# A longer first product after side work, and other places for two sets of split weights, in a two-layer decoder kernel on one core

## The chip, the cores and the metric

The kernel runs on one core of a Trainium2 chip. The metric is the device time of one execution in microseconds (us), as the median of several runs. The core has a matrix engine (PE in the profile; its loading of the stationary operand is a row of its own, PEld), a vector engine (DVE), a scalar engine (ACT), GpSimd (POOL), a queue that issues transfers (SP), and 16 DMA engines. The engines run their own instruction streams and wait for one another by semaphores.

## The reference

A sequence of 256 tokens of width 2048 goes through two layers. Each is a mixer followed by a layer norm over a scaled residual.

```
layer 0 (state space):   z, xBC, dt = split(x @ w_in)           # 2048 -> 4096 + 6144 + 64
                         xBC = silu(causal_conv4(xBC)); xs, B, C = split(xBC)
                         y = chunked scan of (xs, dt, B, C), 8 groups of 8 heads of 64; + d_skip * xs
                         h = group_rms_norm(y * silu(z)) @ w_out  # 4096 -> 2048
layer 1 (sparse attn):   c_q 512, c_kv 256, k_idx 64, w_idx 16, gate 4096 = split(x @ w_in)
                         rms-normed c_q -> 32 query heads, and 16 index heads; top 64 keys per token
                         latent attention over the chosen rows of c_kv; o * silu(gate) @ w_out
x = layer_norm(4**0.25 * x + h) after each layer
```

All is in float32. Nothing of this is changed.

## The kernel before, in words

**Products in three parts.** Each float32 matrix is split into two halves of precision, hi and lo, in a type that the matrix engine takes in one pass. A product a·w is then three products: hi·hi, hi·lo, lo·hi. Weights come from memory in blocks of 128 rows by up to 1024 columns ("units"). For each unit SP issues one transfer into `raw`, ACT copies it to `hi` (L109), DVE subtracts to get `lo` (L131), and PE multiplies. `Stream.run` goes through the list of units in order: it has the unit four ahead converted, calls the unit's `pe`, and then lets each running piece of side work take one step. So the order of the program is written out by hand: a unit's products, then one step of each side piece, then the next unit.

**Where the split weights lie.** `Stream.places` takes a buffer of 1088 columns for hi and one for lo, in rotation over four, and hands out a part of it. Units whose weights stay in the array (`STILL`) start at column 16 (64 bytes); units whose weights are streamed through it (`MOVING`) start at column 0; `KEYS` units have two halves with a gap. `homes` gives single units buffers from another pool and a column to start at. The last four units of the program have `homes` at column 48 (192 bytes).

**The projections by `stream_w`.** The input projection of layer 0 (tile `acc`, moving operand `xT`) and the gates of layer 1 (tile `g`, moving operand `x1T`) have two units for each block of 128 output columns. For each unit the stationary operand is a 128x128 piece of hi or lo, and the moving operand is 256 columns (all tokens): 16 products with hi (L321; hi and lo of the activations alternate) and 8 with lo (L317). The hi and lo activations of one row block lie side by side, 256 columns each. The result tile has 512 columns, of which 256 are used. One group of layer 0 has 10 blocks, so 20 units.

**The side work on PE.** Between units stand short float32 products: the transposed step sizes (`p_dtt`, L291 and L294, once), B·C (`cb`, L365 and L366), transposes of the channel tiles (`pxs`, L416), the scan's outputs (`y`, L436, by `y_steps`, two halves per group), and the mean squares (`ms`, L464). In layer 1 they are the transposes of the normed latents (`qt`, `kvt`, L759), of the index key (`kdt`, L780), index scores (`sa`, `sb`), logits (`lg`), their transposes (`pt`) and outputs (`o`). With `y` of half 0 of a group a run of 10 units follows without side work; with `cb`, `pxs` and `y` of half 1 one of 5.

**Latents.** `stream_tok` multiplies tokens by the 512 columns of c_q (`qp`) and by the 336 of c_kv, k_idx and w_idx (`kvp`, L690 to L692; weights moving). A `kvp` unit holds two row blocks of 336 columns, one behind the other: the second begins 1344 bytes after the first.

**The end.** The output projection (`o`, L537 to L539, 512 columns wide) holds its last 8 units back for the second half of the tokens. The last four of these are done in two passes of 256 columns, into `o` and `part`; then two short sums (`c`, L1210 and L1213) and four vector operations end the program.

Of the kernel before, what the change touches and what calls it, by code (L numbers as in the profile page):

```python
# [17 lines left out]
T = 256  # L18
# [38 lines left out]

MOVING, STILL, KEYS = range(3)  # L60


class Unit:
# [6 lines left out]
class Stream:  # L70


    def __init__(self, nc, wraw, whi, wlo):
        self.nc, self.wraw, self.whi, self.wlo = nc, wraw, whi, wlo
        self.units, self.starts, self.active, self.behind = [], {}, [], []
        self.raws, self.parts, self.halfway = {}, {}, {}
        self.pos = self.ready = 0
        self.limit = 1 << 30
        self.homes = {}

    def add(self, src, width, pe, use):
        self.units.append(Unit(src, width, pe, use))
# [13 lines left out]
    def convert(self, i, eng, later=False):  # L96

        if i < len(self.units):
            u = self.units[i]
            r = self.raws.pop(i)  # L100
            h, l = self.places(i)
            r = r[:, :u.width]
            if u.use == KEYS:
                r = r.rearrange("p (a b) -> p a b", a=2)
            elif i == 0:
                self.nc.scalar.activation(h[:, 0:512], r[:, 0:512], AF.Copy)  # L106
                self.nc.scalar.activation(h[:, 512:1024], r[:, 512:1024], AF.Copy)
            if i:
                self.nc.scalar.activation(h, r, AF.Copy)  # L109
            self.halfway[i] = l, r, h.bitcast(F32)  # L110
            self.parts[i] = (h, l)
        if not later:
            self.finish(i, eng)

    def places(self, i):

        u = self.units[i]
        if i in self.homes:
            pool, o = self.homes[i]
            t = [pool.tile([P, 1088], F32R, tag=k, name=f"{k}{i}") for k in ("hi", "lo")]  # L120
        else:
            o = 16 if u.use == STILL else 0
            t = [pool.tile([P, 1088], F32R, tag=k, name=f"{k}{i}")
                 for pool, k in ((self.whi, "hi"), (self.wlo, "lo"))]
        if u.use == KEYS:
            return [a.rearrange("p (a b) -> p a b", a=2)[:, :, 32:544] for a in t]
        return [a[:, o:o + u.width] for a in t]

    def finish(self, i, eng):
# [34 lines left out]
def trunk_kernel(ctx: ExitStack, tc: tile.TileContext, x, xt, w1, wdt, dtp, prm, wo1,  # L164
                 wkv, wcq, wix, wg, wab, wo2, lnr, out):
    nc = tc.nc
# [21 lines left out]
    def m_tile(name):  # L188
        return p_m.tile([P, 512], F32, tag="m", name=name)
# [68 lines left out]
    def dt_steps():  # L258
# [28 lines left out]
        nc.gpsimd.dma_start(acs_d, acs)  # L287
        yield
        yield
        pt = m_tile("p_dtt")  # L290
        nc.tensor.transpose(pt[:, 0:P], dtT, ident)  # L291
        for h in range(2):
# [10 lines left out]
    def stream_w(half, cell, name, turn=True):  # L303


        def pe(h, l):
            if half == 0:
                cell["ps"] = acc_tile(name)[:, 0:T]
            ps, xs = cell["ps"], cell["x"][0]
            first, second = (1, 0) if half and turn else (0, 1)  # L310
            for lo in (first, second):
                for k in range(8):
                    kt = half * 8 + k
                    last = half == 1 and lo == second and k == 7
                    wt = (l if lo else h)[:, k * P:(k + 1) * P]
                    if lo:
                        nc.tensor.matmul(ps, wt, xs[:, kt, 0:T], start=False,  # L317
                                         stop=last, skip_group_check=True)
                    else:
                        for c in range(2):  # L320
                            nc.tensor.matmul(ps, wt, xs[:, kt, c * T:(c + 1) * T],  # L321
                                             start=(kt == 0 and c == 0), stop=last and c == 1,
                                             skip_group_check=True)
        return pe

    G = [dict() for _ in range(NG)]
# [1 line left out]

    def conv_steps(g, kind, ci, cc, cell):

        ps = cell["ps"]
        acc = sp3.tile([P, T], F32, tag="cacc", name=f"ca{cc}")

        def w(k):
            return convh[:, cc * 5 + k:cc * 5 + k + 1]
        nc.scalar.activation(acc, ps, AF.Identity, scale=w(3), bias=w(4))
        yield
        for k in (2, 1, 0):
            d = 3 - k
            v.scalar_tensor_tensor(acc[:, d:], ps[:, :T - d], w(k), acc[:, d:],  # L340
                                   op0=ALU.mult, op1=ALU.add)
        yield
        if kind == "x":
            dst = sp2.tile([P, T], F32, tag="xs", name=f"xs{g}_{ci}", bufs=12)
        else:
            dst = sp1.tile([P, T], F32, tag=kind, name=f"{kind}{g}")
        nc.scalar.activation(dst, acc, AF.Tanh)
        yield
        v.scalar_tensor_tensor(dst, dst, 1.0, acc, op0=ALU.add, op1=ALU.mult)
        G[g][(kind, ci)] = dst  # L350
        yield

    def z_steps(g, ci, cell):
        ps = cell["ps"]
        zs = sp2.tile([P, T], F32, tag="zs", name=f"zs{g}_{ci}", bufs=4)
        nc.scalar.activation(zs, ps, AF.Tanh, scale=0.5)
        yield
        v.scalar_tensor_tensor(zs, zs, 1.0, ps, op0=ALU.add, op1=ALU.mult)
        G[g][("z", ci)] = zs
        yield  # L360
# [48 lines left out]
    def xst_steps(g, half):  # L409

        xsT = sp2.tile([P, 2, 2, P], F32, tag="xsT", name=f"xsT{g}_{half}")
        pm = m_tile(f"pxs{g}_{half}")
        for c in (0, 1):
            for s in (0, 1):
# [10 lines left out]

    def y_steps(g, half):

        py = y_tile(f"y{g}_{half}")
        xsT = G[g][("xsT", half)]
        ms = [G[g].pop(("M", 2 * half + c)) for c in (0, 1)]  # L430
# [220 lines left out]
    v.tensor_scalar_mul(convh, convh, 0.5)  # L651
    st.run(n_ssd + 27)
    ssd.close()


    d1 = ctx.enter_context(tc.tile_pool(name="d1", bufs=1))
# [24 lines left out]
    def stream_tok(kb, width, cell, name, held=None):  # L681

        def mm(kb, h, l, half):
            ps = cell["ps"][half][:, 0:width]
            for k in range(2):
                kt = kb * 2 + k
                ah = X1[0][:, kt, half * P:(half + 1) * P]
                al = X1[0][:, kt, T + half * P:T + (half + 1) * P]
                hs, ls = h[:, k * width:(k + 1) * width], l[:, k * width:(k + 1) * width]
                nc.tensor.matmul(ps, ah, hs, start=(kt == 0), stop=False)  # L690
                nc.tensor.matmul(ps, ah, ls, start=False, stop=False)
                nc.tensor.matmul(ps, al, hs, start=False, stop=(kt == 15))  # L692
# [17 lines left out]
    GT = {}  # L710

    def gate_steps(h, cell):
        ps, d2 = cell["ps"], L["d2"]
        if h < 16:
            g = A["gates"][h]
        else:
# [16 lines left out]
    def lat_norm(cell, width, g0, nt, name, dst):  # L733
# [17 lines left out]
        yield  # L751
        yield
        for q in range(nt // 2):
            pm = m_tile(f"{name}t{q}")
            for k in range(2):
                for half in range(2):
# [13 lines left out]
    def kidx_steps(cell):  # L770
# [4 lines left out]
            v.tensor_copy(kd[:, :, k * 64:(k + 1) * 64], tok[:, :, 256:320])  # L775
        yield
        yield
        pm = m_tile("kdt")
        for half in range(2):
            nc.tensor.transpose(pm[:, half * P:(half + 1) * P], kd[:, half, :], ident)  # L780
# [8 lines left out]
                                             held if kb < EARLY else None), MOVING)  # L789
    st.side(i, (lat_norm, cells["q"], 512, PC_QG, 4, "q", "cqT"))  # L790
    for kb in range(8):
        i = st.add(wkv[kb], 672, stream_tok(kb, 336, cells["kv"], "kvp"), MOVING)
    st.side(i, (lat_norm, cells["kv"], 256, PC_KVG, 2, "kv", "ckvT"))
    st.side(i, (kidx_steps, cells["kv"]))
    gates = iter(range(NH2))
# [461 lines left out]
    heads.close()  # L1257
    wmore = ctx.enter_context(tc.tile_pool(name="wlast", bufs=4))
    for i in range(len(st.units) - 4, len(st.units)):
        st.homes[i] = wmore, 48  # L1260
    st.run(len(st.units))
    st.drain()

# [80 lines left out]
```

## Time and profile before

| | |
|---|---|
| runs | 1232.03, 1232.05, 1232.72 us; median 1232.05 |
| the profiled execution | 1232.59 us, of which the span from first to last instruction is 1230.3 us |
| DMA queue of the weights | 215.29 MB, 54.7% of 16 engines' span |
| DVE L131, the lo halves | 404 instructions, 491.7 us |
| ACT L109, the hi halves | 403 instructions, 421.8 us |
| PE L321 and L317 into `acc` | 2560 and 1280 products, 477.7 us busy |
| PE L321 and L317 into `g` | 1024 and 512 products, 196.9 us busy |

A row of the timeline gives the start in us from the span's start, the length, engine, line and operation, out<-in, the shape (weights, then moving operand) and how many instructions are merged. Products are pipelined: the length of one is more than its step, so the time of a product is read from the difference of two starts, divided by the count between them. The windows view gives the busy time of each engine in a stretch.

### The profile page before, as it was taken

Reading aid. Unit: us, or ns where it says so; the run is one execution under the profiler, and the core shown is the slowest. Engines: PE = TensorE matmul, PEld = TensorE weight load, DVE = VectorE, ACT = ScalarE, POOL = GpSimd, SP = SyncE. Lnnn points to the kernel's source line nnn. Section 1 sums busy time; section 2 is a strip of 40 time slices with the busy share of each in tenths; the row PEclk is TensorE's granted clock in tenths of the full one; section 3 lists DMA queues with packets and bytes.
Section 4 is the critical chain, followed back from the end, with each engine's and each line's share of the span. In section 5 each row is a group of like instructions: output and inputs, shape, how many; then the busy total and the mean of one; then the engine's idle time right before and its main releaser. Section 6 shows DMA issues by size and latency. Waiting matters only on the chain.

```text
span 1230.3 us, 22861 instructions
## 1 busy us (share of the span) xinstructions
PE 1224.1 (99%) x8981; PEld 1141.6 (93%) x8981; DVE 902.9 (73%) x1644; ACT 667.7 (54%) x1163; POOL 65.1 (5%) x102
## 2 busy tenths in 40 slices
PE   9999999999999999999999999999999999999998
PEld 8999999999999999888888899999999999888886
DVE  7878787887888888756556767877777777567457
ACT  5555555665566556444335655566666666433441
POOL 0001011001100110110000000000000001000000
PEclk9999999999999999999999999999999999999999
DMA  8665566566656665667656564554544555875662
GB/s 296 226 187 192 192 196 196 168 217 194 192 174 208 202 193 175 190 212 245 196 193 205 184 216 148 179 172 155 163 149 154 168 156 186 314 228 186 200 195 94
DMA packets 65370, 236.75 MB, mean 192 GB/s; under 512 B 8024, under 2 KB 8160, under 8 KB 64880
## 3 DMA queue, kind: packets, MB, share of 16 engines
q1 hardware_dynamic: 60352, 215.29, 54.7%
q0 software_dynamic: 4912, 20.02, 4.9%
q8 instruction: 70, 1.15, 0.4%
q14 instruction: 36, 0.29, 0.1%
HBM read 231.00 MB, written 4.28 MB: 191 GB/s over the span
## 4 chain that ended last, share of the span: by engine, by line
PE 99%; DMA 1%; DVE 0%; SPq 0%; ACT 0%; DVEq 0%; issue 0%
PE acc L321 24%; PE acc L317 12%; PE g L321 10%; PE o L537 9%; PE o L538 9%; PE o L539 9%; PE g L317 5%; PE y L436 2%; PE q L892 1%; PE q L894 1%; PE q L893 1%; PE pt L957 1%; PE v L880 1%; PE v L881 1%; PE v L879 1%; PE k L870 1%
## 5 line engine op out<-in xcount | busy, mean ns | idle before, releaser
L131 DVE TENSOR_TENSOR lo<-raw,hi 128x1024 fp32r<-128x1024 f32 (+1 forms) x404 | 491.7, 1220 | 271.7 <-ACT hi L109 270.8
L109 ACT ACTIVATE hi<-raw 128x1024 fp32r<-128x1024 f32 (+1 forms) x403 | 421.8, 1051 | 214.9 <-PE o L539 157.4
L321 PE MATMUL acc<-xT,hi 128*128 128x256 f32 x2560 | 314.2, 279 | 0.2 <-ACT hi L106 0.2
L321 PEld LDWEIGHTS acc<-xT,hi 128*128 128x128 f32 x2560 | 303.3, 188 | 3.3 <-ACT E L391 1.2
L317 PE MATMUL acc<-xT,lo 128*128 128x256 f32 x1280 | 163.5, 279 | 0.0
L317 PEld LDWEIGHTS acc<-xT,lo 128*128 128x128 f32 x1280 | 154.7, 188 | 0.1
L321 PE MATMUL g<-x1T,hi 128*128 128x256 f32 x1024 | 126.7, 278 | 0.0
L321 PEld LDWEIGHTS g<-x1T,hi 128*128 128x128 f32 x1024 | 120.7, 188 | 0.2
L537 PE MATMUL o<-hi,yg 128*128 128x512 f32 x256 | 100.3, 392 | 0.0
L537 PE MATMUL o<-hi,og 128*128 128x512 f32 (+1 forms) x256 | 99.7, 389 | 0.0
L539 PE MATMUL o<-hi,yg 128*128 128x512 f32 x256 | 99.7, 389 | 0.0
L538 PE MATMUL o<-lo,yg 128*128 128x512 f32 x256 | 99.6, 389 | 0.0
L539 PE MATMUL o<-hi,og 128*128 128x512 f32 (+1 forms) x256 | 98.9, 386 | 0.0
L538 PE MATMUL o<-lo,og 128*128 128x512 f32 (+1 forms) x256 | 98.8, 386 | 0.0
L340 DVE SCALAR_TENSOR_TENSOR ca<-acc,par,ca 128x255 f32<-128x255 f32 x144 | 69.0, 479 | 3.4
L317 PE MATMUL g<-x1T,lo 128*128 128x256 f32 x512 | 70.2, 281 | 0.0
L317 PEld LDWEIGHTS g<-x1T,lo 128*128 128x128 f32 x512 | 62.9, 188 | 0.2
L537 PEld LDWEIGHTS o<-hi,yg 128*128 128x128 f32 x256 | 48.1, 188 | 10.2 <-ACT hi L109 0.2
L539 PEld LDWEIGHTS o<-hi,yg 128*128 128x128 f32 x256 | 48.0, 188 | 10.1
L538 PEld LDWEIGHTS o<-lo,yg 128*128 128x128 f32 x256 | 48.1, 188 | 9.7
L539 PEld LDWEIGHTS o<-hi,og 128*128 128x128 f32 x256 | 48.1, 188 | 9.7
L538 PEld LDWEIGHTS o<-lo,og 128*128 128x128 f32 x256 | 48.1, 188 | 9.6
(270 smaller groups left out, 1660.6 us busy)
## 6 DMA issues: line engine op xcount, KB each, us to landing
raw<-in_w_dram SPq DMA_DIRECT2D x160, 512.0 KB, 3.8
raw<-in_wo_dram SPq DMA_DIRECT2D x128, 512.0 KB, 4.2
raw<-in_wg_dram SPq DMA_DIRECT2D x64, 512.0 KB, 3.5
raw<-in_wab_dram SPq DMA_DIRECT2D x32, 512.0 KB, 3.5
abc<-acs_d POOLq DMA_DIRECT2D x32, 256.0 KB, 4.2
raw<-in_wcq_dram SPq DMA_DIRECT2D x8, 512.0 KB, 4.5
raw<-in_wkv_dram SPq DMA_DIRECT2D x8, 336.0 KB, 3.3
scr<-in_xt_dram SPq DMA_DIRECT2D x4, 512.0 KB, 6.3
```

The lines of the kernel that those rows point to most:

```text
L109: self.nc.scalar.activation(h, r, AF.Copy)
L131: eng.tensor_sub(*self.halfway.pop(i))
L317: nc.tensor.matmul(ps, wt, xs[:, kt, 0:T], start=False, stop=last, skip_group_check=True)
L321: nc.tensor.matmul(ps, wt, xs[:, kt, c * T:(c + 1) * T], start=(kt == 0 and c == 0), stop=last and c == 1, skip_group_check=True)
L340: v.scalar_tensor_tensor(acc[:, d:], ps[:, :T - d], w(k), acc[:, d:], op0=ALU.mult, op1=ALU.add)
L436: nc.tensor.matmul(py[ks, c * T + s * P:(c + 1) * T], xsT[:, s, c, ks], ms[c][k][:, ws], start=(c == 0 and s == 0), stop=(s == 1), skip_gr ...
L537: nc.tensor.matmul(ps, ah, hs, start=(kk == 2 * first), stop=False)
L538: nc.tensor.matmul(ps, ah, ls, start=False, stop=False)
L539: nc.tensor.matmul(ps, al, hs, start=False, stop=(kk == 31))
L870: nc.tensor.matmul(ps, h[:, 0, o:o + P], ckvT[:, ct, 0:T], start=(ct == 0), stop=False)
L879: nc.tensor.matmul(ps, ch, h[:, 1, o:o + T], start=(ct == 0), stop=False)
L880: nc.tensor.matmul(ps, ch, l[:, 1, o:o + T], start=False, stop=False)
```

## The change

A field `wide` of the stream tells `stream_w` how many columns the next unit's first product takes on top of its 256; it is used once and set back to 0. Pieces of side work set it: 16 at the program's start and behind `p_dtt`, 96 behind every `y` and behind the first `pxs` of group 0 (0 behind any other `pxs`), 64 when layer 0's pools are closed and behind `qt`, `kvt` and `kdt`. The longer product reads on into the columns that lie behind its operand and writes into columns of the result tile that nothing reads; only its first 256 columns are used, as before.

The `kvp` units get a kind of their own, `TWO`: the two row blocks start at bytes 64 and 1472 of the buffer in place of 0 and 1344. The last four units start at byte 0 of their home in place of 192.

```
+MOVING, STILL, KEYS, TWO = range(4)
...
+        self.wide = 16
...
-            if u.use == KEYS:
+            if u.use in (KEYS, TWO):
                 r = r.rearrange("p (a b) -> p a b", a=2)
...
+        if u.use == TWO:
+            return [a[:, o + 16:o + 720].rearrange("p (a b) -> p a b", a=2)[:, :, 0:336] for a in t]
...
     def dt_steps():
...
+        st.wide = 16
         pt = m_tile("p_dtt")
...
         def pe(h, l):
             if half == 0:
-                cell["ps"] = acc_tile(name)[:, 0:T]
+                cell["ps"] = acc_tile(name)
             ps, xs = cell["ps"], cell["x"][0]
             first, second = (1, 0) if half and turn else (0, 1)
+            n, st.wide = T + st.wide, 0
             for lo in (first, second):
                 for k in range(8):
                     kt = half * 8 + k
                     last = half == 1 and lo == second and k == 7
                     wt = (l if lo else h)[:, k * P:(k + 1) * P]
-                    if lo:
-                        nc.tensor.matmul(ps, wt, xs[:, kt, 0:T], start=False,
-                                         stop=last, skip_group_check=True)
-                    else:
-                        for c in range(2):
-                            nc.tensor.matmul(ps, wt, xs[:, kt, c * T:(c + 1) * T],
-                                             start=(kt == 0 and c == 0), stop=last and c == 1,
-                                             skip_group_check=True)
+                    for c in (range(1) if lo else range(2)):
+                        nc.tensor.matmul(ps[:, 0:n], wt, xs[:, kt, c * T:c * T + n],
+                                         start=(kt == 0 and not lo and c == 0),
+                                         stop=last and c == (1 - lo), skip_group_check=True)
+                        n = T
...
     def xst_steps(g, half):
...
+        st.wide = 96 if g == half == 0 else 0
...
     def y_steps(g, half):
+        st.wide = 96
...
     ssd.close()
+    st.wide = 64
...
     def stream_tok(kb, width, cell, name, held=None):
...
-                hs, ls = h[:, k * width:(k + 1) * width], l[:, k * width:(k + 1) * width]
+                hs, ls = (w[:, k * 512:(k + 1) * 512] if width == 512 else w[:, k, :]
+                          for w in (h, l))
...
         for q in range(nt // 2):
+            st.wide = 64
             pm = m_tile(f"{name}t{q}")
...
+        st.wide = 64
         pm = m_tile("kdt")
...
-        i = st.add(wkv[kb], 672, stream_tok(kb, 336, cells["kv"], "kvp"), MOVING)
+        i = st.add(wkv[kb], 672, stream_tok(kb, 336, cells["kv"], "kvp"), TWO)
...
-        st.homes[i] = wmore, 48
+        st.homes[i] = wmore, 0
```

No instruction changes its engine or its place. In all 19 products get longer: 14 behind `y` and one behind `pxs` by 96 columns, two by 64, two by 16. On PE, the place behind `y` of half 0 of group 0 reads as follows before. `y` is the scan's output tile; `acc` is a block of the input projection, and the hi and lo tiles are split weights.

```order
L436 MATMUL y_0_1095<-M_802,xsT_0_720 64x128
L436 MATMUL y_0_1095<-M_982,xsT_0_720 64x256
L436 MATMUL y_0_1095<-M_984,xsT_0_720 64x256
L436 MATMUL y_0_1095<-M_982,xsT_0_720 64x128
L436 MATMUL y_0_1095<-M_984,xsT_0_720 64x128
L321 MATMUL acc_1110<-xT,hi_989 128x256 x16
L317 MATMUL acc_1110<-xT,lo_990 128x256 x8
```

The same place on PE in the changed kernel:

```order
L440 MATMUL y_0_1095<-M_802,xsT_0_720 64x128
L440 MATMUL y_0_1095<-M_982,xsT_0_720 64x256
L440 MATMUL y_0_1095<-M_984,xsT_0_720 64x256
L440 MATMUL y_0_1095<-M_982,xsT_0_720 64x128
L440 MATMUL y_0_1095<-M_984,xsT_0_720 64x128
L322 MATMUL acc_1110<-xT,hi_989 128x352
L322 MATMUL acc_1110<-xT,hi_989 128x256 x15
L322 MATMUL acc_1110<-xT,lo_990 128x256 x8
```

One product of the sixteen is 352 columns wide; the rest stands as it did. On PE at the start of layer 1's gates, behind the `kvp` products and behind `kdt`, before:

```order
L692 MATMUL kvp_8219<-hi_8324,x1T 128x336
L321 MATMUL g_8419<-x1T,hi_8347 128x256 x16
L317 MATMUL g_8419<-x1T,lo_8348 128x256 x8
L317 MATMUL g_8419<-x1T,lo_8370 128x256 x8
L321 MATMUL g_8419<-x1T,hi_8369 128x256 x16
L321 MATMUL g_8501<-x1T,hi_8387 128x256 x16
L317 MATMUL g_8501<-x1T,lo_8388 128x256 x8
L759 MATMUL kvt_8526<-ident,sC 128x128 x4
L780 MATMUL kdt<-ident,sC 128x128 x2
L317 MATMUL g_8501<-x1T,lo_8414 128x256 x8
```

The same place on PE in the changed kernel:

```order
L698 MATMUL kvp_8219<-hi_8324,x1T 128x336
L322 MATMUL g_8419<-x1T,hi_8347 128x320
L322 MATMUL g_8419<-x1T,hi_8347 128x256 x15
L322 MATMUL g_8419<-x1T,lo_8348 128x256 x8
L322 MATMUL g_8419<-x1T,lo_8370 128x256 x8
L322 MATMUL g_8419<-x1T,hi_8369 128x256 x16
L322 MATMUL g_8501<-x1T,hi_8387 128x256 x16
L322 MATMUL g_8501<-x1T,lo_8388 128x256 x8
L766 MATMUL kvt_8526<-ident,sC 128x128 x4
L788 MATMUL kdt<-ident,sC 128x128 x2
L322 MATMUL g_8501<-x1T,lo_8414 128x320
L322 MATMUL g_8501<-x1T,lo_8414 128x256 x7
```

The first product of each of the two runs of gates is 320 columns wide, the second of them one with a lo half.

More of the change, by code (lines that the diff above doesn't have):

```diff
@@ L55 @@
 AHEAD = 2
-MOVING, STILL, KEYS = range(3)
+MOVING, STILL, KEYS, TWO = range(4)
 class Unit:
@@ L329, in conv_steps @@
     def conv_steps(g, kind, ci, cc, cell):
-        ps = cell["ps"]
+        ps = cell["ps"][:, 0:T]
         acc = sp3.tile([P, T], F32, tag="cacc", name=f"ca{cc}")
@@ L353, in z_steps @@
     def z_steps(g, ci, cell):
-        ps = cell["ps"]
+        ps = cell["ps"][:, 0:T]
         zs = sp2.tile([P, T], F32, tag="zs", name=f"zs{g}_{ci}", bufs=4)
@@ L712, in gate_steps @@
     def gate_steps(h, cell):
-        ps, d2 = cell["ps"], L["d2"]
+        ps, d2 = cell["ps"][:, 0:T], L["d2"]
         if h < 16:
```

## The prediction

> **What bounds the kernel now.** I read the page first: busy times, the granted clock, the chain that ended last.
>
> ```profile
> span 1230.3 us, 22861 instructions
> PE 1224.1 (99%) x8981; PEld 1141.6 (93%) x8981; DVE 902.9 (73%) x1644; ACT 667.7 (54%) x1163; POOL 65.1 (5%) x102
> ...
> PEclk9999999999999999999999999999999999999999
> ...
> PE 99%; DMA 1%; DVE 0%; SPq 0%; ACT 0%; DVEq 0%; issue 0%
> ```
>
> PE is the whole chain, at full clock in every slice. So next I read the view of waits, for PE alone; the numbers are total us, times, longest.
>
> ```profile
> PE zeros L626 <- DVE scr L621: 1.3, 1, 1.3
> PE acc L321 <- ACT hi L106: 0.2, 1, 0.2
> PE lg L930 <- DVE mx L941: 0.2, 1, 0.2
> ```
>
> PE waits 1.7 us in all, most of it at the start. What can change the time is therefore how many products there are and what step each takes. A busy PE does not show the step, so the third view is the timeline of PE, over one half group of layer 0.
>
> ```profile
> 78.53 1.98 PE L321 MATMUL acc<-xT,hi 128*128 128x256 f32 x16
> 80.43 1.52 PE L436 MATMUL y<-M,xsT 128*64 128x256 f32 x16
> 81.88 2.15 PE L321 MATMUL acc<-xT,hi 128*128 128x256 f32 x16
> ...
> 85.76 3.93 PE L321 MATMUL acc<-xT,hi 128*128 128x256 f32 x32
> 89.53 2.05 PE L317 MATMUL acc<-xT,lo 128*128 128x256 f32 x16
> ...
> 108.37 2.05 PE L321 MATMUL acc<-xT,hi 128*128 128x256 f32 x16
> 110.26 0.59 PE L365 MATMUL cb<-C,B 128*128 128x256 f32 x2
> ...
> 111.44 1.52 PE L436 MATMUL y<-M,xsT 128*64 128x256 f32 x16
> 112.89 2.10 PE L321 MATMUL acc<-xT,hi 128*128 128x256 f32 x16
> ...
> 116.63 3.79 PE L321 MATMUL acc<-xT,hi 128*128 128x256 f32 x32
> 120.26 1.98 PE L317 MATMUL acc<-xT,lo 128*128 128x256 f32 x16
> ```
>
> The same shape runs at two steps. Behind the first `y`: (89.53 − 85.76) / 32 = 117.8 ns. Behind the second: (120.26 − 116.63) / 32 = 113.4 ns. Lengths show it too, 3.93 against 3.79 us for 32. The step does not drift: it is 2.05 for 16 at 108.37 as at 89.53, through all four buffers, and changes only where something of another kind stood on PE. Both starts come behind the same 16 `y` products. The windows view tells that no other engine is what differs; its columns are the length and the busy times of PE, PEld, DVE, ACT, POOL, then clock, DMA share and GB/s.
>
> ```profile
> 81.88:110.26 28.38, 28.38 (x243) 28.38 (x242) 24.14 (x40) 17.09 (x27) 2.27 (x3) 1.00 0.61 195
> 112.89:126.61 13.72, 13.72 (x122) 13.72 (x121) 11.13 (x17) 7.24 (x12) 2.95 (x3) 1.00 0.57 185
> 127.39:141.18 13.79, 13.79 (x123) 13.67 (x121) 9.14 (x14) 6.01 (x9) 0.55 (x1) 1.00 0.62 206
> 142.64:171.01 28.37, 28.37 (x242) 28.37 (x241) 24.13 (x40) 17.05 (x27) 2.20 (x3) 1.00 0.61 194
> ```
>
> A stretch of 240 products at the long step takes 28.38 us, and the next group's 28.37; two of 120 at the short step take 13.72 and 13.79. DVE, ACT, clock and transfers look alike in both. So the step is set on PE itself, by how the run of products starts, and then holds. That is what the longer first product touches.
>
> **The change part by part.** The sum is made against the profiled execution, 1232.59 us; the median of the runs is 0.5 us below it.
>
> *The price of a column.* The end of the program has the same operands 512 and 256 wide:
>
> ```profile
> 1208.40 0.39 PE L537 MATMUL o<-hi,og 128*128 128x512 f32 x1
> ...
> 1211.12 0.39 PE L537 MATMUL o<-hi,og 128*128 128x512 f32 x1
> ...
> 1214.07 0.28 PE L539 MATMUL o<-hi,og 128*128 128x256 f32 x1
> ...
> 1219.47 0.28 PE L539 MATMUL part<-hi,og 128*128 128x256 f32 x1
> ```
>
> (1211.12 − 1208.40) / 12 = 226.7 ns, and (1219.47 − 1214.07) / 45 = 120.0 ns. The 256 extra columns cost 106.7 ns, 0.417 ns each: 96 cost 40 ns, 64 cost 27, 16 cost 7. Nothing hides them, as PE is the chain.
>
> *Behind `y` of half 0, groups 0 to 6: seven stretches of 240 at the long step (117.8 ns, below the slow step; 113.4 is the fast one).* At the fast step such a stretch takes 13.72 us (120 products with their start) and 120 × 113.4 ns = 13.61 us more, so 27.33 us in place of 28.38. Less 0.04 for the columns, 1.01 us each: **−7.07 us**. Whether a first product that is 40 ns longer starts the run at the fast step is the unknown of this case, and the trace of before has no such product. From below it is worth the 7.07 us; from above nothing, and seven times 0.04 us lost. I take the fast step. What speaks for it: the slow step comes from the start alone, the longer product moves what follows against what stood ahead, and the rows in this text show ten kinds of start, of which six land at the short step. Three of these are behind `p_dtt`, `sa` and `lg`:
>
> ```profile
> 43.81 3.79 PE L321 MATMUL acc<-xT,hi 128*128 128x256 f32 x32
> ...
> 758.97 3.79 PE L321 MATMUL g<-x1T,hi 128*128 128x256 f32 x32
> ...
> 798.39 3.79 PE L321 MATMUL g<-x1T,hi 128*128 128x256 f32 x32
> ```
>
> The others at 113.4 ns are behind `y` at 112.89 and behind `pxs` at 66.64 and 127.39; at 117.8 ns are those behind `y` at 81.88, `pxs` at 52.07, `kvp` and `kdt`. So I start from six in ten, and go a little above, since the load of the next weights has more time under a longer product.
>
> *Behind `y` of half 1: seven stretches of 120, fast already.* If they stay so, 7 × 0.04: **+0.28 us**. If they fall to the slow step, 120 × 4.4 ns = 0.53 us each, +3.7 us more.
>
> *Behind the first `pxs`, and behind `p_dtt` and at the start.*
>
> ```profile
> 52.07 2.13 PE L321 MATMUL acc<-xT,hi 128*128 128x256 f32 x16
> ...
> 66.29 0.60 PE L416 MATMUL pxs<-ident,xs 128*128 128x128 f32 x4
> 66.64 1.17 PE L317 MATMUL acc<-xT,lo 128*128 128x256 f32 x8
> ```
>
> From 52.07 to 66.29 a stretch of 120 takes 14.22 us; the fast one behind the next `pxs`, 66.64 to 80.43, takes 13.79. With 0.04 for columns: **−0.39 us**, or +0.04 if it stays. The two products with 16 columns more cost **+0.01 us**.
>
> *The gates.*
>
> ```profile
> 698.19 0.31 PE L690 MATMUL kvp<-hi,x1T 128*128 128x336 f32 x1
> ...
> 703.69 0.60 PE L759 MATMUL qt<-ident,sC 128*128 128x128 f32 x4
> ...
> 713.79 2.04 PE L321 MATMUL g<-x1T,hi 128*128 128x256 f32 x16
> ...
> 722.27 0.60 PE L759 MATMUL kvt<-ident,sC 128*128 128x128 f32 x4
> ...
> 722.85 1.19 PE L317 MATMUL g<-x1T,lo 128*128 128x256 f32 x8
> ...
> 731.41 0.28 PE L807 MATMUL ix<-cqT,hi 128*128 128x256 f32 x1
> ...
> 739.98 0.48 PE L826 MATMUL sa<-sC 64*128 64x256 f32 x1
> ```
>
> 72 products from 713.79 to 722.27 take 8.48 us, 117.8 ns each, and 72 from 722.85 to 731.41 take 8.56: both slow. The 72 of `ix` that follow without a break keep that step (739.98 − 731.41 = 8.57 us). At the fast step each 72 save 72 × 4.4 ns = 0.32 us; two of them pay 0.03 for columns: **−0.90 us**, or +0.05 if nothing switches.
>
> *The latents' places.* From 698.19 to 703.69 stand 36 `kvp` products: 152.8 ns each, where 336 columns at 0.417 ns are 140.0. So 12.8 ns each are lost, 96 products, 1.2 us at most. A 256-wide product loses 6.7 ns at the fast step, 11.1 at the slow. Half of the `kvp` products, those at byte 64, get a place that the second blocks have now, 1344 being 64 beyond a multiple of 256; I cost them at nothing. The others get byte 1472, whose distance to a moving operand at a multiple of 256 is the streams' own 64 bytes. If these fall to the loss of the fast step, 48 × 6.1 ns: **−0.3 us**. Bounds: 96 × 6.1 = −0.6, and +0.3 if it goes the other way.
>
> *The last four units' place.* 48 products of 256 columns take 120.0 ns, which is 6.6 above the fast step. Bounds: 48 × 6.6 ns = −0.3, and +0.3 if the 24 that are 512 wide lose another 13 ns. The rows say that place matters there and not which one is good: I take **0**. A gain would reach the end, since DVE waits there for PE:
>
> ```profile
> 1219.79 0.42 DVE L1245 TENSOR_TENSOR fin<-fin,part 128x256 f32<-128x256 f32 x1 [1.17 <-PE part L539]
> ```
>
> The Trainium skill weighs against the two edits of place: SBUF — State Buffer, Who interferes with whom, gives PE two independent read ports, one for weights and one for the moving operand. By that where an operand lies is worth nothing, and both terms are 0. The trace does not quite agree: 120.0 ns at the end and 113.4 in the stretches are one shape at one clock.
>
> *Sum:* −7.07 + 0.28 − 0.39 + 0.01 − 0.90 − 0.3 + 0 = −8.4 us. 1232.6 − 8.4 = 1224.2 against the profiled execution, 1223.7 against the median; I say 1224.0. What is late next: DVE has 24.1 us of work in a slow stretch. In 27.4 us that is 88%, against 85% now and 81% in the fast stretch at 112.89, where PE waited for nothing; conversion runs four units, some 11 us, ahead.
>
> **The rivals.**
>
> *Nothing switches.* The columns only cost: 14 × 0.04 + 0.04 + 0.05 + 0.01 = 0.67 us, with the two places at −0.3: 1233.0 against the profiled execution, 1232.4 against the median. For it: the longer product ends its extra columns with no load beside it, and what follows it could meet the same conditions. Against it: two equal `y` pieces already lead to two steps. [...]
>
> *Half 0 gets fast, half 1 slow.* −8.4 + 3.7 = −4.7 us: 1227.9. The first runs then end differently, so the second ones start otherwise than now; no row shows how.
>
> *Slower: the longer start lands slow everywhere behind `y`.* The seven runs of 120 lose 3.7 us, nothing is gained: 1233.0 + 3.7 = 1236.7. It decides as soon as more than half of the products behind `y` that are fast today turn slow while the 240s stay. For it: behind `kvp`, itself wider than 256, the run at 713.79 is slow. Against it: only `kvp` tells it.
>
> *DVE becomes the bound of layer 0* and gives back half: 1228. Against it stand the 81% above without a wait.
>
> *The change does not do what it says.* A later piece could overwrite `wide`; the order of instructions has 352 columns behind every `y`, so no.
>
> **How the numbers follow.** Forecast 0.56; half 1 slow 0.12; DVE 0.03; nothing switches 0.21; slower 0.08. A measurement of this kernel tells about 0.2%, 2.5 us, from no change. So faster 0.56 + 0.12 + 0.03 = 0.71, same 0.21, slower 0.08. The forecast's own range is 1222.9 to 1226; with the case of nothing switched up to 1233.2 it holds about nine in ten of these cases, and without it under eight.
>
> **What would show it.** Right: the 32 products at 85.76 take 3.79 and not 3.93 us, the 240 some 27.4 us, the gates 8.2 us. Wrong in the first term: 3.93 still stands there. Wrong in the second: 3.93 in the stretch behind `cb`, `pxs` and `y`. DVE: a row of PE waiting for `lo`. Places: `kvp` steps other than 152.8 ns, the last 48 other than 120.0.

## The result, and the profile after

The changed kernel takes 1225.74 us, median of four runs (1224.61 to 1226.91), against 1232.3 us for the kernel before in the same rounds (1232.03 to 1232.72): a ratio of 0.9947, interval 0.9929 to 0.9964. A second set of five runs beside other kernels gave 1225.12 us (1224.96 to 1226.43), ratio 0.9944, interval 0.9930 to 0.9957. So it is faster by 6.6 us in the first set and by 7.5 in the second, some 7 of the 8.4 us that the sum gave.

The page of the changed kernel says again that PE is everything:

```profile
span 1224.9 us, 22862 instructions
...
PE 1216.4 (99%) x8981; PEld 1133.9 (93%) x8981; DVE 902.7 (74%) x1644; ACT 667.0 (54%) x1163; POOL 64.9 (5%) x102
```

The number of products, 8981, is that of before, and the busy time has shrunk by 7.7 us. Which step the products take is read in the timeline of PE, over the same half group as before:

```profile
80.58 1.52 PE L440 MATMUL y<-M,xsT 128*64 128x256 f32 x16
82.03 2.14 PE L322 MATMUL acc<-xT,hi 128*128 128x352 f32 x16
84.01 1.98 PE L322 MATMUL acc<-xT,lo 128*128 128x256 f32 x16
85.82 3.79 PE L322 MATMUL acc<-xT,hi 128*128 128x256 f32 x32
89.45 1.98 PE L322 MATMUL acc<-xT,lo 128*128 128x256 f32 x16
...
109.40 0.59 PE L367 MATMUL cb<-C,B 128*128 128x256 f32 x2
...
110.58 1.52 PE L440 MATMUL y<-M,xsT 128*64 128x256 f32 x16
112.03 2.13 PE L322 MATMUL acc<-xT,hi 128*128 128x352 f32 x16
114.00 1.98 PE L322 MATMUL acc<-xT,lo 128*128 128x256 f32 x16
115.81 3.79 PE L322 MATMUL acc<-xT,hi 128*128 128x256 f32 x32
```

The row at 82.03 shows the wide first product (352 columns). Where 3.93 us stood for 32 products, 3.79 stands: (89.45 − 85.82) / 32 = 113.4 ns, the short step of the prediction, in place of 117.8, the long one. The 240 products from 82.03 to 109.40 take 27.37 us, where 28.38 stood. The stretch of half 1, at 112.03, had the short step and keeps it. The windows view has both, with the stretch of the next group:

```profile
82.01:109.38 27.37, 27.37 (x242) 27.35 (x241) 23.21 (x39) 16.34 (x26) 2.26 (x3) 1.00 0.59 192
112.01:125.77 13.76, 13.76 (x122) 13.74 (x121) 11.49 (x16) 7.75 (x14) 2.95 (x3) 1.00 0.63 202
141.80:169.17 27.37, 27.37 (x242) 27.35 (x241) 23.21 (x39) 16.34 (x26) 2.20 (x3) 1.00 0.61 192
```

DVE has 23.2 us of work in 27.37 (85%), and PE has no wait for a `lo`. Behind the first `pxs`, the 120 products from 52.70 to 66.44 take 13.74 us, 0.48 less than before:

```profile
52.70 2.11 PE L322 MATMUL acc<-xT,hi 128*128 128x352 f32 x16
...
66.44 0.60 PE L419 MATMUL pxs<-ident,xs 128*128 128x128 f32 x4
```

The gates did not follow:

```profile
707.24 2.07 PE L322 MATMUL g<-x1T,hi 128*128 128x320 f32 x16
...
711.03 3.93 PE L322 MATMUL g<-x1T,hi 128*128 128x256 f32 x32
...
715.75 0.60 PE L766 MATMUL kvt<-ident,sC 128*128 128x128 f32 x4
...
716.32 1.22 PE L322 MATMUL g<-x1T,lo 128*128 128x320 f32 x8
717.38 3.93 PE L322 MATMUL g<-x1T,hi 128*128 128x256 f32 x32
...
724.91 0.28 PE L815 MATMUL ix<-cqT,hi 128*128 128x256 f32 x1
```

The wide product (320) is there twice, and behind it stands 3.93: the 72 products take 8.51 and 8.59 us, 0.03 more each than before. Below, the totals of stretches are taken in this way, from the start of the first product to the start of what follows it.

Two things in this one execution are not the change's. PE's waits have two new rows at the start, and a longer third one (0.2 us before):

```profile
PE p_dt L619 <- DMA scr<-in_wdt_dram: 0.6, 1, 0.6
PE p_dt L619 <- DMA scr<-in_xt_dram: 0.5, 1, 0.5
PE acc L322 <- ACT hi L107: 0.5, 1, 0.5
```

The first projection product starts at 9.84 us against 9.21. In the fourteen profiles of this case that start lies between 9.07 and 9.84 us, whatever the edit. And from the start of the last PE instruction to the end of the span 6.0 us pass, against 4.9 before and 4.9 in the second profile of the changed kernel. Between those two points, from the start of the first projection product to the start of the last PE instruction, the changed kernel takes 1209.08 us (1209.09 in its second profile) against 1216.18: −7.1 us. That is what the change did; the rest is start and end.

### The profile page after: what moved, and what is told of

It is laid out like the page before. It is cut to its first block, busy times and chain, and to the rows that moved or that the text cites. A ratio compares the mean times of both kernels' runs of the same rounds, so it can differ in the third digit from the quotient of the medians.

```text
span 1224.9 us, 22862 instructions
## 1 busy us (share of the span) xinstructions
PE 1216.4 (99%) x8981; PEld 1133.9 (93%) x8981; DVE 902.7 (74%) x1644; ACT 667.0 (54%) x1163; POOL 64.9 (5%) x102
## 4 chain that ended last, share of the span: by engine, by line
PE 99%; DMA 1%; DVE 0%; SPq 0%; ACT 0%; DVEq 0%; issue 0%
PE acc L322 36%; PE g L322 14%; PE o L541 9%; PE o L543 9%; PE o L542 9%; PE y L440 2%; PE q L900 1%; PE q L901 1%; PE q L902 1%; PE pt L965 1%; PE v L888 1%; PE v L889 1%; PE v L887 1%; PE k L878 1%; PE k L879 1%; PE k L880 1%
## 5 line engine op out<-in xcount | busy, mean ns | idle before, releaser
L322 PE MATMUL acc<-xT,hi 128*128 128x256 f32 (+1 forms) x2560 | 309.6, 277 | 0.5 <-ACT hi L107 0.5
L322 PEld LDWEIGHTS acc<-xT,hi 128*128 128x128 f32 x2560 | 298.9, 188 | 3.5 <-issue 1.4
L322 PE MATMUL acc<-xT,lo 128*128 128x256 f32 x1280 | 160.8, 277 | 0.0
L322 PEld LDWEIGHTS acc<-xT,lo 128*128 128x128 f32 x1280 | 152.2, 188 | 0.1
L322 PE MATMUL g<-x1T,hi 128*128 128x256 f32 (+1 forms) x1024 | 126.7, 278 | 0.0
L349 ACT ACTIVATE xs<-ca 128x256 f32<-128x256 f32 x32 | 13.4, 419 | 80.6 <-DVE ca L342 47.1
```

The lines of the kernel that those rows point to most:

```text
L322: nc.tensor.matmul(ps[:, 0:n], wt, xs[:, kt, c * T:c * T + n], start=(kt == 0 and not lo and c == 0), stop=last and c == (1 - lo), skip_gr ...
```

## The experiments

Twelve kernels were run, the last of them the changed kernel again. The short diffs are against the changed kernel, unless said otherwise, and are cut to the lines that matter. "The 240s" are the seven stretches of 240 products behind `y` of half 0; a stretch, or run of products, is "short" at the 113.3 ns step and "long" at the 117.8 ns step.

**1. The wide product behind `y` alone.** The kernel before with 96 columns behind every `y`, and nothing else of the change. The diff shows three of the places that are set back.

```
-        self.wide = 16
+        self.wide = 0
...
-        st.wide = 64
...
-    st.homes[i] = wmore, 0
+    st.homes[i] = wmore, 48
```

> The kernel before with one part of the change: the first product behind every y is 96 columns wider; places, gates, first pxs and the 16s are as before. If the seven runs of 240 behind y of half 0 carry the gain: each takes 27.37 us and not 28.37, each run of 120 behind half 1 takes 13.76 and not 13.72, sum 7 x 1.007 - 7 x 0.041 = 6.8 us below before, about 1225.5; the first pxs run stays at 14.22. Rival, the gain needs the first pxs run at the short step too, since the state is handed on from run to run: then some of the seven stay at 28.37 and the time is above 1226.5.

Measured: 1226.12 us (1224.42 to 1226.55), ratio 0.9943, interval 0.9927 to 0.9960. The seven 240s take 27.367 us, the first `pxs` run 14.219 as before, the gates 8.482 and 8.563. So the edit behind `y` carries the gain, and all others together are worth little: between the two points named above this kernel takes 1209.3 us, the whole change 1209.1.

**2. The change without that edit.** `st.wide = 96` behind `y` becomes 0. The edit took it from both halves, not from half 0 alone.

```
-        st.wide = 96
+        st.wide = 0
```

> The change without the widening behind y of half 0 (width 0 there), all else as changed. If each run's step is set by its own first product: seven runs at 28.37 again, 7.05 us above the changed kernel's span, 1232 us of span at the same start and end; the first pxs run stays at 13.74. Rival, the states are handed on: runs of 240 behind a y whose forerunner now ends elsewhere could be short anyway, fewer than seven at 28.37.

Measured: 1233.53 us in a single execution. The gain is gone: between the two points 1215.8 us, against 1216.2 in the kernel before. The seven 240s are back at 28.373 us. The stretches of half 1 take 13.722 us, short without a wide product too; so there the 96 columns only cost 0.04.

**3. How wide it must be.** Behind half 0, one width for each group.

```
-        st.wide = 96
+        st.wide = 96 if half else (0, 16, 32, 48, 64, 80, 128, 0)[g]
```

> The change with another width in each group behind y of half 0: 0, 16, 32, 48, 64, 80, 128 columns for groups 0 to 6 (96 behind half 1 as changed). Theory one, a longer first product gives the next weights' load time: all widths above some threshold give the short step (27.3 us a run), all below it the long one (28.4). Theory two, the extra columns move the run against something that repeats every 64 columns: 32 short like 96; 0, 64 and 128 long. Theory three, any longer product will do: only 0 is long.

Measured: 1228.15 us. By width 0, 16, 32, 48, 64, 80 and 128 the 240s take 28.373, 27.340, 28.390, 28.397, 27.367, 27.360 and 27.374 us. Two rows of the timeline for 32 columns, and two for 64 (the second row of each is what tells):

```profile
201.99 2.17 PE L322 MATMUL acc<-xT,hi 128*128 128x288 f32 x16
204.00 2.05 PE L322 MATMUL acc<-xT,lo 128*128 128x256 f32 x16
...
323.65 2.14 PE L322 MATMUL acc<-xT,hi 128*128 128x320 f32 x16
325.63 1.98 PE L322 MATMUL acc<-xT,lo 128*128 128x256 f32 x16
```

16 columns do it, 32 and 48 do not. No theory on record had this: neither a threshold, nor something that repeats every 64 columns, nor any width at all. The idea of the prediction, that a longer product gives the next weight load time, falls with it, as 32 gives more time than 16.

**4. Where it must stand.** Per group: third product 96 wider; fifth product 96; the last product but one *ahead of* `y` 96, the first plain; an extra 96-column product ahead; first product 8, 4 and 256 wider.

```
+            at, more, lead = EXTRA.get((name, half), (0, st.wide, 0))
...
+                        n = T + (more if i == at else 0)
+                        i += 1
```

> The change with other means behind y of half 0, one in each group: group 0 third product 96 wider in place of the first; group 1 fifth product; group 2 the last but one product ahead of y; group 3 an extra product of 96 columns of its own ahead of the run (an addition to columns that nothing reads); group 4 first product 8 wider; group 5 first product 4 wider; group 6 first product 256 wider. If what counts is more time under the first load alone: groups 0, 1, 2 and 3 long (28.4 us), 6 short, 4 and 5 long. If any shift of the run's start counts: groups 2 and 3 short too. If a longer product resets the run wherever it stands: groups 0 and 1 short from there on, 27.4 to 27.5 us.

Measured: 27.381, 27.380, 28.374, 27.447 (241 products), 27.334, 27.340 and 27.433 us. A longer product inside the run does it as well; one ahead of `y` does nothing. And 4 columns, 1.7 ns, are enough. So it takes no delay of the run's start, and a delay of `y` and the run together does not do it.

**5 and 6. Stretches still at the long step.** In the changed kernel four were chosen: the 216 products behind `p_dt` (25.55 us), the 24 behind `ms`, and the two runs of 72 gates, of which the second is followed by `ix`. Two kernels, with different widths and places:

```
+    EXTRA = {("acc1", 1): (0, 16, 0), ("acc159", 1): (0, 8, 0),
+             ("g0", 0): (4, 8, 0), ("g1", 1): (3, 16, 0)}
...
+    EXTRA = {("acc1", 1): (4, 8, 0), ("acc159", 1): (3, 96, 0),
+             ("g0", 0): (0, 4, 0), ("g1", 1): (0, 16, 0)}
```

> Changed kernel, with a longer product in the four stretches that still run at the long step (117.8 ns). Behind p_dt, unit 1 half 1: first product 16 columns wider. Behind ms, unit 159: first product 8 wider. First 72 of the gates: not the first but the fifth product wider, by 8 (the 64 of the first go). Second 72: the fourth by 16 (the 64 of the first go). If a longer product sets the run anew wherever it stands: the 216 behind p_dt go from 25.55 to about 24.6 us, the 24 behind ms from 3.02 to 2.91, each 72 of the gates from 8.51 and 8.59 to about 8.2 and 8.3, and ix behind the second from 12.36 to about 12.0: some 1.9 us in all. If what stands in the gates' operands or ahead of them holds the long step there (64 did nothing): only the first two change, 1.0 us in all, and the gates stay at 117.8 ns. If each place needs a width of its own, some switch and some do not, with no rule by this run alone.

> The same four stretches with other longer products. Behind p_dt: the fifth product 8 wider; behind ms: the fourth 96 wider; first 72 of the gates: first product 4 wider in place of 64; second 72: first product 16 wider in place of 64. If a longer product sets the run anew with a chance of landing short that depends on width and place: some of the four switch here that do not in the run beside it, and the other way round. If 4 and 8 always do and 64 in the gates was a bad width: all four are short, 1.9 us less than the changed kernel. If the gates cannot be switched: 8.5 and 8.6 us stand again whatever the width.

Measured: 1223.78 and 1224.12 us. The 216 behind `p_dt` take 24.62 and 24.61, short in both. In the second kernel, though, this run began short before its wider fifth product: its first four steps are 220, 114, 113 and 113 ns. Behind `ms`, 8 columns on the first product changed nothing (3.02 us); 96 on the fourth gave the short step behind it (2.98). The gates take 8.19 and 8.29 us in the first kernel, 8.49 and 8.57 in the second. The profile of the first, at the gates, shows something else too:

```profile
706.09 2.00 PE L331 MATMUL g<-x1T,hi 128*128 128x256 f32 x16
707.93 1.98 PE L331 MATMUL g<-x1T,lo 128*128 128x256 f32 x16
```

Starts of the first products, from the trace, are 117, 116, 114 and 113 ns apart: the run was at the short step *before* its fifth, wider product. What had gone there were the 64 columns of the first.

**7. Places for the 512-wide products.** Weights of the first output projection at eight places, eight units (96 products) each.

```
+            if 160 <= i < 224:
+                o = (0, 16, 32, 48, 8, 24, 56, 4)[(i - 160) // 8]
```

> Changed kernel, with the weights of the first output projection (units 160 to 223, products 512 wide, 48 per eight units) put at 0, 64, 128, 192, 32, 96, 224 and 16 bytes past their buffers' start, eight units each; the held operand stays at a multiple of 256. If what counts is how far held and moving operand lie apart within 256 bytes, as in the streams where 64 apart is the place of 113.3 ns: the eight units at 192 (48 products) take a step of about 220 ns, those at 0 stay at 226.7, and those at 64 take the 229 ns that the last four units have since the change. If the 512 wide products do not follow the streams' places: 226.7 ns or more at all eight, and the run is level with or slower than the changed kernel. In time: at most 48 x 7 ns = 0.3 us either way, so the steps decide and not the total.

Measured: 1230.2 us; between the two points 3.6 us more than the changed kernel. There are 96 products at each place and not 48 as the expectation had it, and seven of the eight places are slower. Only place 0 keeps 226.7 ns. Places 192, 32, 96 and 224 bytes hold the 384 products from 557.34 to 646.94:

```profile
557.34 0.40 PE L543 MATMUL o<-hi,yg 128*128 128x512 f32 x1
...
646.94 0.40 PE L543 MATMUL o<-hi,yg 128*128 128x512 f32 x1
```

89.60 us / 384 = 233.3 ns. At 64 bytes it is about 229, at 16 and 128 about 232. So 192, the distance at which the 256-wide streams have their 113.3 ns, is no good place for products of 512; the theory of a common distance falls. As the groups follow each other, part of a step may have been carried on from one to the next. The Trainium skill, SBUF — State Buffer, Who interferes with whom, gives PE two independent read ports; read as the prediction reads it, a place is worth nothing, and these steps disagree.

**8. The wide product inside the run.** Behind `y`, in the gates, behind `ms` and behind `p_dt` it is now a later product and not the first; in every second head pair the third of the twelve `v` products is 8 columns wider.

```
+    EXTRA = {("acc24", 0): (4, 32, 0), ("acc44", 0): (4, 48, 0), ("acc64", 0): (8, 32, 0),
+             ("acc84", 0): (8, 48, 0), ("acc104", 0): (12, 4, 0), ("acc124", 0): (20, 16, 0),
+             ("acc144", 0): (6, 128, 0), ("g0", 0): (8, 32, 0), ("g1", 1): (10, 48, 0),
+             ("acc159", 1): (5, 48, 0), ("acc1", 1): (8, 32, 0)}
...
+                    n = T + (8 if s == ct == 0 and VWIDE(p) else 0)
```

> Changed kernel, with the longer product inside the run and not at its start. Behind y of half 0, groups 1 to 7 (counted from 0: the runs that begin at units 24, 44, 64, 84, 104, 124, 144): fifth product 32 wider, fifth 48, ninth 32, ninth 48, thirteenth 4, twenty-first 16, seventh 128. Gates: ninth product 32, in the second 72 the eleventh 48. Behind ms: sixth 48; behind p_dt: ninth 32. In the head pairs the third v product 8 wider in every second pair (0, 2, 4, ...), not in the others. Theory A (a longer product sets a run anew to the short step wherever it has products of its own kind ahead of it; only at the start of a run can it miss): all of them start at 117.8 ns and go to 113.3 behind the wide product, 32 and 48 too, which missed as first products: the seven runs 27.33 to 27.46 us, p_dt's 24.65, gates about 8.25 and 8.35. Theory B (the width decides, 32 and 48 are bad anywhere): runs with 32 and 48 stay at 28.39, 8.5 and 8.6 us, those with 4, 16 and 128 switch. Theory C (each hit was a chance of some seven in ten): two to four of the eleven stay long. The v products: if their 117.8 ns are the same long step, the nine behind the wide one go to 113.3 in every second pair, 0.04 us each; if it is the price of their place, they stay at 117.8 as in the pairs between.

Measured: 1226.07 us. 32 and 48 as fifth product: 28.383 and 28.390, long. As ninth product: 27.387 and 27.380, short. The other three: 27.400, 27.420 and 27.420, short from the wide product on. Behind `p_dt`: 24.669, short. Behind `ms`, 48 as sixth: long. The timeline of the first and the third:

```profile
83.12 2.05 PE L333 MATMUL acc<-xT,lo 128*128 128x256 f32 x16
85.00 3.93 PE L333 MATMUL acc<-xT,hi 128*128 128x256 f32 x32
...
204.76 1.98 PE L333 MATMUL acc<-xT,lo 128*128 128x256 f32 x16
206.57 3.79 PE L333 MATMUL acc<-xT,hi 128*128 128x256 f32 x32
```

So neither A nor B holds: the same 32 columns miss at the start and at the fifth product and hit at the ninth. C gets its number of misses, but not its chance, as the next run shows. The gates began short again, before their wide products; those cost 0.03 to 0.05 us there and left the run short. In the pairs with the wide `v`, the last six of the twelve take 113 ns; 1398 ns in place of some 1420, about 20 ns a pair. Their long step is the same one, not a price of the place. Pairs 0 and 1 are short in the changed kernel without it (1379 ns), and there the wide product only costs 20 ns.

**9. Chance or rule.** The widths changed among the groups, half 1 plain, gates plain.

```
-        st.wide = 96
+        st.wide = 0 if half else (32, 48, 16, 4, 32, 48, 8, 0)[g]
...
-    st.wide = 64
+    st.wide = 0
```

> Changed kernel with other widths of the first product: behind y of half 0, groups 0 to 6, 32, 48, 16, 4, 32, 48 and 8 columns; behind every y of half 1 none; in the gates none (the 64 of all their first products go), while the latents' weights stay in two pieces. If width at this place decides in a fixed manner (32 and 48 missed behind groups 2 and 3, while 4, 8 and 16 hit behind 5, 4 and 1): the four stretches with 32 and 48 stay at 28.39 us and the three with 16, 4 and 8 take 27.34. If it is chance or the group: about seven in ten are short whatever the width, so that one or more of the four with 32 and 48 come short, or one with 4, 8 or 16 stays long. Half 1 without a wider product: 13.72 us each (short), or 14.24 if it needs it behind a short 240. Gates: in the two runs in which their first product was plain (places in two pieces, a wider product only later) they began at the short step; if it is the plain start that does it, 8.18, 8.26 and 12.0 us (ix) here, 1.0 us less than in the changed kernel; if it was the later wider product, 8.5, 8.6 and 12.4 as in the kernel before. Total by the first theory: 4.0 us lost in four stretches, 0.5 won in columns and 1.0 in the gates, so about 2.5 us above the changed kernel.

Measured: 1227.99 us. 32 and 48 columns: 28.390, 28.396, 28.390, 28.397. 16, 4 and 8: 27.339, 27.340, 27.333. With run 3 that is six misses of six for 32 and 48, whatever the group. So it is fixed by the program, and not chance. Half 1 takes 13.72 to 13.73 us, short. The gates:

```profile
710.45 1.98 PE L322 MATMUL g<-x1T,hi 128*128 128x256 f32 x16
...
714.08 3.79 PE L322 MATMUL g<-x1T,hi 128*128 128x256 f32 x32
...
720.20 3.79 PE L322 MATMUL g<-x1T,hi 128*128 128x256 f32 x32
```

8.17 and 8.26 us, short, with nothing wide in them. The 96 `ix` products take 11.17 us in place of 11.51 (the 12.36 and 12.0 of the expectation have the `sa` products among them).

**10 to 12. What the runs add up to, and why plain gates are short.** A kernel put together; the same with the latents' weights in one piece again; and the changed kernel once more. The first has run 9's plain gates, 8 columns behind `y` of half 0, none behind half 1, and

```
+    EXTRA = {("acc1", 1): (4, 8, 0), ("acc159", 1): (3, 96, 0)}
...
+    VWIDE = lambda p: True
```

The second is the first with

```
-        i = st.add(wkv[kb], 672, stream_tok(kb, 336, cells["kv"], "kvp"), TWO)
+        i = st.add(wkv[kb], 672, stream_tok(kb, 336, cells["kv"], "kvp"), MOVING)
```

> Changed kernel, put together from what the runs showed: first product behind y of half 0 8 columns wider, behind half 1 none; gates none; behind p_dt the fifth product 8 wider; behind ms the fourth 96 wider; in each head pair the third v product 8 wider. The latents' weights stay in two pieces, the last four units at their new place. From the stretches measured one by one: p_dt 25.55 to 24.61, gates and ix 25.68 to 24.68, y half 0 7 x 0.03, half 1 7 x 0.04, ms 0.04, v 16 x 0.02: about 2.8 us below the changed kernel, 1222.9 us if that is at 1225.7, 0.992 of the kernel before. If the stretches hang on each other through the step at which the one ahead ends, one or more of them land long again: 1224 to 1227.

> The kernel put together, with the latents' weights in one piece again, as in the kernel before. If the two pieces are what lets plain gates begin at the short step: gates 8.48 and 8.56 us and ix 12.36 here, against 8.17, 8.26 and 11.99, so 1.0 us more. If it is something else ahead of them (the wider products of layer 0): 8.17 and 8.26 here too. The 96 kvp products: 0.1 us shorter.

> The changed kernel itself once more, beside the one put together on the same chip. Its stretches as in its first profile: seven 240s at 27.37 us, 216 behind p_dt at 25.55, gates 8.51 and 8.59, if what sets the step is fixed by the program; if it is chance, one or more of these differ. Time 1224.6 to 1226.9 as before; the first stream product between 8.9 and 10 us of the span, by when the first transfers land.

Measured: the kernel put together 1223.04 us (1222.83 to 1223.24, five runs), ratio to before 0.9925, interval 0.9912 to 0.9937; the changed kernel 1225.12 beside it. Between the two points it takes 1206.5 us, 2.6 less than the changed kernel; 2.8 were expected. Each stretch came out as when it was measured alone, within 0.03 us. Here the run behind `p_dt` began long and went short behind its wider fifth product. In the changed kernel's second profile every stretch was as in its first, within 0.01 us.

The second kernel tells the cause in the gates: one edit, the latents' places. First its rows, then those of the kernel put together:

```profile
705.39 2.04 PE L330 MATMUL g<-x1T,hi 128*128 128x256 f32 x16
...
709.16 3.93 PE L330 MATMUL g<-x1T,hi 128*128 128x256 f32 x32
...
715.47 3.93 PE L330 MATMUL g<-x1T,hi 128*128 128x256 f32 x32
```

```profile
705.50 1.98 PE L330 MATMUL g<-x1T,hi 128*128 128x256 f32 x16
...
709.13 3.79 PE L330 MATMUL g<-x1T,hi 128*128 128x256 f32 x32
...
715.25 3.79 PE L330 MATMUL g<-x1T,hi 128*128 128x256 f32 x32
```

With the weights in one piece the gates take 8.48 and 8.56 us, in two pieces 8.17 and 8.26; the 96 `ix` products go along (11.50 and 11.17). The `kvp` products themselves are 0.08 us longer in two pieces. By these stretches the two pieces are worth 0.9 us, through what stands behind them, and the change's 64 columns undo it. Between the two points the difference is 0.94 us (1206.46 against 1207.41); 0.09 of it is the program's first run of 24 products, which was long in the second kernel's profile, with the same instructions.

## Why the prediction was right, and where it was not

- *PE's step is set on PE itself, by how a run starts, and holds.* Right for the stretches that carry the gain: all seven 240s switched and stayed, while clock and transfers look alike in the windows. It is not the whole: a longer product inside the run sets it too (runs 4 and 8).
- *Half 0, −7.07 us.* Right: 7 × (27.367 − 28.373) = −7.04 us, 1.01 each. That these starts would land at the short step was taken as a chance of about six in ten, so it was in part luck: of the ten widths that runs 1, 3, 4 and 9 had as first product there, eight gave the gain, and 32 and 48 columns nothing.
- *The reason given for the chance, more time for the next weight load.* Wrong: 4 columns do it and 32 do not (runs 3, 4 and 9).
- *Half 1, +0.28 us.* Right: 13.763 us a stretch against 13.722, +0.29 over seven. The rival in which half 1 goes long fell.
- *First `pxs`, −0.39; the 16 columns, +0.01.* The first measured −0.48: the short stretch taken for it, behind the second `pxs`, begins a little slower (13.79 against 13.74). The 16 columns measured +0.00: +0.01 behind `p_dtt`, and the first run of the program varies by as much.
- *Gates, −0.90 us.* This step failed: "At the fast step each 72 save 72 × 4.4 ns". The gates stayed long, +0.03 us for each 72, +0.07 with `ix`. It took for granted that the wide product decides alone. A plain start behind the latents' new place gives the short step, and 64, 16 or 4 columns behind the same place give the long one (the changed kernel, run 6).
- *Latents' places, −0.3 us.* The step failed too: measured +0.08. The first 36 of the 336-wide products went from 152.8 to 154.4 ns and not to the loss of the fast step; what the edit could bring lies behind them.
- *Last four units, 0.* Right, as a sum of two signs. The 48 products of 256 columns went from 120.0 to 117.8 ns (5.75 to 5.65 us); the 512-wide ones ahead of them rose from 226.7 to about 230 ns over 36 products (+0.12). Together +0.02 us. Only the first 24 of these 36 have the new place; the next 12, at the old one, kept the longer step and then fell back to 226.7 ns with nothing wide among them. So a step of 512-wide products can end without an edit.
- *DVE as the bound.* Fell: 85% busy, and PE waits for no `lo`.
- *The sum.* Measured by stretches: −7.04 + 0.29 − 0.48 + 0.00 + 0.07 + 0.08 + 0.02 = −7.1 us, as is what lies between the first projection product and the last PE instruction. The two terms that failed are 1.3 us of the 1.7 between 1224.0 and 1225.74; the rest is less than the start of an execution varies by (0.8 us over the profiles).

Left open is why 4, 8, 16, 64, 80, 96, 128 and 256 columns set the run anew at its start and 32 and 48 do not, and why these do at the ninth product. At the start the two misses lie next to each other among the widths tried (16 and 64 are their neighbours); no run had a width between. Open too is why a longer first product takes the gates from the short step to the long one. What a width does behind `y` is the same in every group and profile where it was tried; no run shows what makes it.

## What to carry to other kernels

Where the matrix engine is the whole chain, compare the step of like products in every stretch: two steps of one shape can mean a gain that no view of waits names. Try several small widths, and several places of the wide product, since one that misses says nothing of the next; and measure each stretch on its own, because an edit in one can decide the step of the one behind it, as the latents' places did for the gates. Leave out the wider product where the run is short already.

## What the runs showed of the hardware that was not expected

- Products of 256 columns with the same operands run for hundreds of products at 113.3 or at 117.8 ns, at a granted clock of 1.00, and a single product 4 columns longer can move them from the long step to the short one.
- A run keeps its step through products of other operands that follow without a break: `ix` has the step of the gates ahead of it in every profile, 113.3 or 117.8 ns.
- Products of 512 columns take 226.7 ns where held and moving operand lie, by their addresses in the program, at the same place within 256 bytes, and 229 to 233 at the seven others tried; the same products with 256 columns took 120.0 at the same place (the end of the kernel before) and 117.8 at 64 bytes from it (the changed kernel); the streams of 256, at 192 bytes, have 113.3 and 117.8.
- The first run of 24 products, 16 columns wider in its first, was short in most profiles (2.94 to 2.95 us) and long (3.03) in two, runs 6 and 11, with the same instructions; there the arrival of the first transfers varies too.
- What stands ahead reaches through side work. Behind the 32 `p_dt` products a run whose first products are plain began long in the eleven profiles in which that first run of 24 was short, and short in the two in which it was long.
